# Attention's PSUM in two pools: the scores' two-bank tiles apart, the one-bank tiles and the product of P and V in one rotation of four

## The chip, the cores and the metric

The kernel runs on one core of a Trainium2 chip. The metric is the device time of one execution in microseconds (us). Five engines work beside each other and meet only at semaphores: TensorE (PE in the profile, with its weight loads as PEld), VectorE (DVE), ScalarE (ACT), GpSimd (POOL) and SyncE (SP), which issues the transfers. Matmuls write their results to PSUM, which the kernel uses as eight banks, each of 128 partitions by 512 fp32 numbers; DVE and ACT carry them from there to SBUF.

## What is computed

One layer of a hybrid block on 1024 latent tokens and 256 context tokens, width 1024, all in fp32. The part that the change touches is the window attention (8 query heads in two groups, blocks of 128 queries, three neighbouring key blocks and the context), which runs woven together with a bidirectional mLSTM and the output projection:

```python
s_loc = jnp.einsum('bnqhgd,bnkhd->bnhgqk', qb, kw).astype(jnp.float32) * scale
s_ctx = jnp.einsum('bnqhgd,bchd->bnhgqc', qb, kc).astype(jnp.float32) * scale
m = jnp.maximum(jnp.maximum(s_loc.max(-1, keepdims=True), s_ctx.max(-1, keepdims=True)), sk)
p_loc = jnp.exp(s_loc - m)
p_ctx = jnp.exp(s_ctx - m)
inv = 1.0 / (p_loc.sum(-1, keepdims=True) + p_ctx.sum(-1, keepdims=True) + jnp.exp(sk - m))
o = (jnp.einsum('bnhgqk,bnkhd->bnqhgd', (p_loc * inv).astype(v.dtype), vw)
     + jnp.einsum('bnhgqc,bchd->bnqhgd', (p_ctx * inv).astype(v.dtype), vc))
...
mix_x = jnp.concatenate([att_x, ml_x], axis=-1) @ w_out[layer]
x = x + gt_m * rms_norm(mix_x, g_post_mix[layer])
fx = swiglu(modulate(rms_norm(x, g_pre_ffn[layer]), sh_f, sc_f), w_ffn_in[layer], w_ffn_out[layer])
x = x + gt_f * rms_norm(fx, g_post_ffn[layer])
```

Before it come the modulation, the input projection and the mLSTM's states; behind it the output projection's rest and the feed-forward part.

## The kernel before

The attention stage runs through 16 items, one for each block of 128 queries (n from 0 to 7) and group of four heads (g 0 and 1). An iteration of the loop at L1038 works on three things at once. It computes the **scores** of the item two ahead (class `Soft`, four calls of `scores`, one a head: four matmuls, L953 and L954 twice, into a tile of tag "s", which takes two banks; DVE's L955 takes the maximum and moves the 512 or 640 columns out; ACT's L964 is the exponential, DVE's L966 the reciprocal, POOL's L969 the scaling). It transposes the **probabilities** of its own item (class `Values`, `tr`, up to five times T0 to T4: four transposes of 128 by 128, L982, fill one bank of tag "pt", which DVE's L985 (odd t) or ACT's L987 (even t) copies to SBUF as `ts_`). And, in the first eight iterations, it does one block of the **mLSTM**: `ml_scores` (L860, a tile of tag "s"), `ml_values` twice (L874 and L878 into two banks of tag "pt", read by DVE's L883 and L884 and by ACT's L890 in the first direction, DVE's L892 in the second), `ml_norm` (ACT, POOL's L902) and `ml_out` (four transposes L908 into a bank of tag "pt", read by DVE's L909). In odd iterations, when both groups' probabilities are transposed, `pv` multiplies them with V (L1000) into the bank `po`, and `pv_out` (ACT's L1006) copies that out. From the sixth iteration on the loop also casts the output weights (ACT's L925, POOL's L926), and at its end the output projection (L75 to L77 into tag "s") begins.

PSUM's eight banks in this stage are one pool: tag "s" has two tiles of two banks, "pt" three banks and "po" one. The product's bank `po` is used by nothing else until the feed-forward part. A tile that is asked for takes a bank of its tag that is free or comes free first, and its first matmul waits for the last reader of the tile that was there.

What stands where in each engine's queue is not written by hand in this stage: the program lists the steps of an iteration in the order of the strings `PLAN_ML`, `PLAN` and `PLAN13` (L35 to L37), and a scheduler then sets the order from its own estimate of when operands and banks are there. With `T` the transposes, `A` scores, `N` exponentials, `V` the values, `z` `ml_out`, `M` the product and `O` its copy:

```python
PLAN_ML = ("T0 A0 A1 A2 A3 T1 T2 T3 V0 N0 T4 z V1 w s N1 x p", "T0 A0 A1 A2 A3 T1 T2 V0 N0 T3 T4 z V1 w s M O N1 x p")
```

Only from the stage's last two items on (L1077 on) and in the whole feed-forward part is the order written by hand. Ahead of the attention, the pool `psA` holds the eight banks of the input projection; the last to leave them are the two halves of a sigmoid on ACT (L776), and `psB` opens in the same banks. The feed-forward part (L1118 on) goes on with tags "s", "pt" and "po".

Of the kernel before, what the change touches and what calls it, by code (L numbers as in the profile page):

```python
# [9 lines left out]
F32 = mybir.dt.float32  # L10
# [3 lines left out]
PSUM = bass.MemoryType.PSUM  # L14
ADD, SUB, MUL, MAX, MIN = ALU.add, ALU.subtract, ALU.mult, ALU.max, ALU.min

P = 128
D = 1024
# [24 lines left out]
def body(tc, x, ctx, vecs, bcv, bada, gqm, gqf, wada, ws1, ws2, wt, wout, wfi, wfo,  # L43
# [5 lines left out]
    def open_pool(name, bufs=1, side="left", space=None):  # L49
        kw = dict(name=name, bufs=bufs, reuse_waits="tile")  # L50
        if space is not None:
            kw["space"] = space
        else:
            kw["side"] = side
        p = tc.tile_pool(**kw)
        return p, p.__enter__()

    def close(p):
        p[0].__exit__(None, None, None)
# [65 lines left out]
    def R(k, name, shape, dt=F32):  # L125
        t = rp[1].tile([P, 1152 if k < 4 else 1024], dt, name=name, tag=f"r{k}")
        n = int(np.prod(shape))
        v = t[:, 0:n]
        if len(shape) == 2:
            v = v.rearrange("p (a b) -> p a b", b=shape[1])  # L130
        elif len(shape) == 3:
            v = v.rearrange("p (a b c) -> p a b c", b=shape[1], c=shape[2])
        elif len(shape) == 4:
            v = v.rearrange("p (a b c d) -> p a b c d", b=shape[1], c=shape[2], d=shape[3])
        return v
# [160 lines left out]
    for sec in (1, 0):  # L296
# [52 lines left out]
        for q in range(2):  # L349
            t = (hcol, scol)[sec][:, q]  # L350
# [70 lines left out]
    for i in range(NI):  # L421
# [16 lines left out]
        if i in (1, 2):  # L438
            b = i - 1
# [138 lines left out]
    def T(i, name):  # L578
        return q2.tile([P, S], F32, name=name, tag=f"s{i}")
# [159 lines left out]
    for j, name in enumerate(TILES):  # L739
# [10 lines left out]
        elif name == "ak":  # L750
# [5 lines left out]
            for a, b, w, dst in ((kr, ks, S, slice(0, S)), (kc[:, 0:L], kc[:, L:2 * L], L, slice(S, S + L))):  # L756
                t = th[64:P] if w == S else kc[64:P, 2 * L:3 * L]
# [7 lines left out]
        elif name.startswith("aq"):  # L765
            t = T(0, f"aq{i}")
# [6 lines left out]
        else:  # L773
            t = R(14 if i == 3 else 15, "so", (S,))
# [39 lines left out]
    pb = psB[1]  # L814
# [4 lines left out]
    qa = atp[1]  # L819
    qa.tile([P, 4, P], F32, name="ts_", tag="pts", bufs=NTS)  # L820
    qa.tile([P, 80], F32, name="padq")
    for x_, n in (("pt", 3), ("po", 1)):
        pb.tile([P, 4, P], F32, name=x_, tag=x_, bufs=n)

    def bank():
        return pb.tile([P, 4, P], F32, name="pt", tag="pt", bufs=3)

    def two_banks():
        return [t.rearrange("p a b -> p (a b)") for t in (bank(), pb.tile([P, 4, P], F32, name="po", tag="po", bufs=1))]


    wts, qps, hss, qz = {}, {}, {}, {}
# [71 lines left out]
    def ml_out(n):  # L904
        hs, so = hss.pop(n)
        pt = bank()
        for h in range(4):
            pe.transpose(pt[:, h, :], hs[:, h, :], ident)  # L908
        dve.tensor_tensor(mix[n][:, 4:8, :], pt, so, MUL)  # L909
# [79 lines left out]
    pos = {}  # L989

    def pv(a, b, ts, more, pin=True):

        ts = [t for t in ts if t < a.nt][::-1]
        first = a.n not in pos
        if first:
            pos[a.n] = pb.tile([P, 4, P], F32, name="po", tag="po", bufs=1)
        for t in ts:
            vt = a.kb0 + t if t < a.nb else NT + t - a.nb
            for g, x_ in ((1, b), (0, a)):
                r = pe.matmul(pos[a.n][64 * g:64 * g + 64], av[:, vt, g], x_.p.pop(t), start=first and t == ts[0],  # L1000
                              stop=not more and t == ts[-1])
                if pin and (t != ts[0] or not g):
                    tc.keep_in_program_order(r)

    def pv_out(n):
        act.copy(mix[n][:, 0:4, :], pos.pop(n))  # L1006
# [3 lines left out]
    for i in range(2):  # L1010
        a = Soft(i)
# [25 lines left out]
    b = None  # L1037
    for i in range(NIT):  # L1038
        a = Soft(i + 2) if i + 2 < NIT else None
        b0, b = b, Values(i)  # L1040
# [5 lines left out]
        for k in (PLAN_ML[i % 2] if i < NT else PLAN13 if i == NIT - 3 else PLAN[i % 2]).split():  # L1046
            op, n = k[0], int(k[1:] or 0)
            if op == "w" and i + 1 < NT:
                ml_load(i + 1)
            elif op == "T" and n < b.nt:  # L1050
                b.tr(n)
            elif op == "M" and i % 2:
                pv(b0, b, range(5), False)
            elif op == "O" and i % 2:
                pv_out(b.n)
            elif op == "A" and a:
                a.scores(n)
            elif op == "N" and a:
                a.norm(n)
            elif op == "V" and i < NT:  # L1060
                ml_values(i, n)
            elif op == "x" and i < NT:
                ml_norm(i)
            elif op == "s" and i + 1 < NT:
                ml_scores(i + 1)
            elif op == "z" and 1 <= i <= NT:
                ml_out(i - 1)
            elif op == "p" and i in WSPLIT:
                wout_split(i)
            elif op == "m":  # L1070
                msplit(0, 0)
                ops_[0] = pb.tile([P, 1024], F32, name="op", tag="s", bufs=2)
            elif op == "P":
                omm(0, 0, range(n, n + 1))
# [17 lines left out]
    msplit(1, 1)  # L1092
    act.preload_act_table_set("sqrt_and_others")
    pv(b, b2, range(4), False, False)
    omm(0, 1, range(3, 4))
    ops_[1] = pb.tile([P, 1024], F32, name="op", tag="s", bufs=2)
    omm(1, 1, range(4))
    pv_out(b.n)
    order.__exit__(None, None, None)
    close(atp)  # L1100
    close(aqp)
    close(akp)
# [142 lines left out]
    def mm_fi(ps, w, b, first):  # L1245

        for k in range(4):
            mm3(ps, (w[:, 0, k], w[:, 1, k]), b[k], first and k == 0, k == 3, more=not first)

    def bop(x):  # L1250
        return [(bh[x][0][:, k], bh[x][1][:, k]) for k in range(4)]

    xv, zb, tm_ = {}, {}, {}

    def fi1(p):
        if p == 2:
            xv[p] = two_banks()
        else:
            t = pb.tile([P, D], F32, name=f"xv{p}", tag="s", bufs=2)
            xv[p] = [t[:, 0:512], t[:, 512:D] if p else pb.tile([P, 512], F32, name="xv0b", tag="po", bufs=1)]  # L1260
        mm_fi(xv[p][0], wops[p]["11"], bop("11"), True)

    def fi2(p):
# [81 lines left out]
    tsums(2, (0, 1))  # L1345
    tsp("T2", 0, 2, "h")
    fi1(0)
    opost1(N1)
    es0 = prp[1].tile([P, 512], F32, name="es0", tag="mh", bufs=2)
# [7 lines left out]
    fi2(0)  # L1357
    xstore(N1)
    fi1(1)
    otr(N1)  # L1360
    close(pC)
# [20 lines left out]
    def fm(p, k):  # L1382

        w = wops[p]
        if k == 1:
            return fi1(p)
        if k == 2:
            return fi2(p)
        X = xv[p][0]
        if k == 6:  # L1390
            mm_fi(X, w["S2"], top("T2"), False)
        elif k == 5:
            zb[p] = bank().rearrange("p a b -> p (a b)")
            mm_fi(zb[p], w["S1"], top("T1"), True)
        elif k == 7:
            mm_fi(X, w["S3"], top("T3"), False)
        elif k == 4:
            mm_fi(X, w["22"], top("T4"), False)
        else:
            mm_fi(zb[p], w["S4"], bop("22"), False)  # L1400
# [95 lines left out]
    def gacc(k):  # L1496

        if k < KT:
            dve.scalar_tensor_tensor(gt["acc"], gt[k], csil[:, k, 0:1], gt["acc"], MUL, ADD)
            return  # L1500
        gps = two_banks()
        for i in range(2):
            sl = slice(i * 512, (i + 1) * 512)
            ps = gps[i]
            for p_ in range(2):
                pe.matmul(ps, gt["one"], gt["hl"][:, p_, sl], start=not p_, stop=p_ == 1)
            gt["p", i] = ps
# [193 lines left out]
    for p in range(4, HT):  # L1701
# [39 lines left out]
        if not end:  # L1741
            fm(p + 1, 1)
        else:
            X4 += two_banks()
            t = pb.tile([P, D], F32, name="fx2", tag="s", bufs=2)
            X4 += [t[:, 0:512], t[:, 512:D]]
            fstep(0)
# [95 lines left out]
    for s_ in range(1, 8):  # L1843
        q0 = (s_ - 1) * NJ
        KL = 4 if s_ == 7 else 2
        if s_ == 2:
            t = pb.tile([P, D], F32, name="fy0", tag="s", bufs=2)
# [35 lines left out]
    close(h2p)  # L1883
    close(prp)
    close(rp)
    close(psB)
    close(cp)

# [79 lines left out]
```

## Time and profile before

| | us |
|---|---|
| three timed runs | 1181.55, 1183.47, 1183.47 (median 1183.47) |
| the profiled execution, its own time | 1182.6 |
| its span from the first to the last instruction | 1180.8 |
| busy in the span: PE, DVE, ACT, POOL | 1161.4, 781.2, 558.2, 154.4 |
| the stage between the first score and the last copy of the product (L1006) | 292.8 to 459 |

Times within the span count from its start. PE starts a matmul before the one ahead of it has left the array, so that the rows of neighbouring matmuls overlap: what a matmul costs is the distance to the next one's start, not its own duration. An arrow in a row (`<-DVE ts__3367 L985`) names the instruction whose end released the waiting one, and the number before it is the idle time. A name such as `ts__3367` is one tile; its number differs between the two kernels by a small shift (before `pt_3369`, after `pt_3372`), as do line numbers behind L823 (before L982, after L987).

### The profile page before, as it was taken

To read this page: it belongs to the slowest core of one execution; us is meant where nothing else is said; L and a number is where in the kernel's file an instruction comes from. 1 tells how busy PE (TensorE), PEld (TensorE's weight loads), DVE (VectorE), ACT (ScalarE), POOL (GpSimd) and SP (SyncE) were. 2 spreads that over 40 slices of the span, in tenths; PEclk is the share of its full clock that TensorE was granted. 3 is DMA by queue.
4 is the path that set the end of the run, shared out by engine and by line. 5 is a ranking of instruction groups with operands and counts; after the bars stand their busy time and mean duration, and the time that the engine had idled before them with its cause. 6 is when DMAs were issued, how large, how long until landed. Compare 5 with 4: busy or idle time off the path is not lost.

```text
span 1180.8 us, 16205 instructions
## 1 busy us (share of the span) xinstructions
PE 1161.4 (98%) x5881; PEld 949.4 (80%) x5881; DVE 781.2 (66%) x1367; ACT 558.2 (47%) x1035; POOL 154.4 (13%) x204
## 2 busy tenths in 40 slices
PE   8899999999999999999999999999999999999997
PEld 3799888777777776888788888888888888888886
DVE  5863768872877752559767767777777755644566
ACT  6743442221776873887533433333333434434543
POOL 1550001225434670000000000000000000000000
PEclk9999999999999999999999999999999999999999
DMA  9611954748764325220333575655654458665853
GB/s 366 218 54 53 380 200 141 216 129 220 215 177 111 113 58 178 82 97 36 98 134 124 206 240 204 224 195 206 216 177 134 179 189 276 205 213 188 304 185 126
DMA packets 100264, 208.59 MB, mean 177 GB/s; under 512 B 9812, under 2 KB 39124, under 8 KB 98776
## 3 DMA queue, kind: packets, MB, share of 16 engines
q1 hardware_dynamic: 100184, 207.56, 52.9%
q8 instruction: 46, 0.75, 0.3%
q14 instruction: 34, 0.28, 0.1%
HBM read 154.04 MB, written 52.83 MB: 175 GB/s over the span
## 4 chain that ended last, share of the span: by engine, by line
PE 86%; DMA 5%; DVE 4%; issue 1%; ACT 1%; POOL 1%; SPq 1%; DVEq 0%; POOLq 0%; ACTq 0%
PE xv L77 8%; PE xv L75 8%; PE xv L76 8%; PE pt L75 6%; PE pt L76 6%; PE pt L77 6%; PE po L1000 3%; PE pt L982 3%; PE op L75 2%; PE op L77 2%; PE op L76 2%; PE t L595 2%; PE t L597 2%; PE t L594 2%; PE fx L75 2%; PE slab L75 2%
## 5 line engine op out<-in xcount | busy, mean ns | idle before, releaser
L64 DVE TENSOR_TENSOR fo<-fr,fo 128x1024 fp32r<-128x1024 f32 x77 | 92.6, 1222 | 69.8 <-ACT fo L63 65.4
L63 ACT CAST fo<-fr 128x1024 fp32r<-128x1024 f32 x77 | 79.7, 1052 | 73.9 <-PE pt L77 33.2
L594 PE MATMUL t<-hh,th 128*128 128x512 f32 x208 | 82.4, 396 | 0.0
L595 PE MATMUL t<-hl,th 128*128 128x512 f32 x208 | 82.1, 395 | 0.0
L1374 ACT CAST wS<-wr 128x512 fp32r<-128x512 f32 x88 | 54.2, 622 | 55.3 <-PE pt L77 36.7
L1376 DVE TENSOR_TENSOR wS<-wr,wS 128x512 fp32r<-128x512 f32 x88 | 60.4, 688 | 19.8 <-ACT wS L1374 19.7
L77 PE MATMUL xv<-tT,wS 128*128 128x512 f32 x168 | 65.7, 391 | 0.0
L75 PE MATMUL xv<-tT,wS 128*128 128x512 f32 x168 | 65.6, 391 | 0.0
L76 PE MATMUL xv<-tT,wS 128*128 128x512 f32 x168 | 65.5, 390 | 0.0
L597 PE MATMUL t<-hh,tl 128*128 128x512 f32 x208 | 65.0, 393 | 0.0
L75 PE MATMUL op<-woh,mh 128*128 128x512 f32 x128 | 51.0, 398 | 0.0
L77 PE MATMUL op<-woh,ml 128*128 128x512 f32 x128 | 49.9, 390 | 0.0
L76 PE MATMUL op<-wol,mh 128*128 128x512 f32 x128 | 49.9, 390 | 0.0
L1122 DVE TENSOR_TENSOR wr<-wr 128x512 f32<-128x512 f32 x66 | 45.5, 689 | 1.4
L594 PEld LDWEIGHTS t<-hh,th 128*128 128x128 f32 x208 | 39.1, 188 | 8.3 <-issue 0.3
L595 PEld LDWEIGHTS t<-hl,th 128*128 128x128 f32 x208 | 39.1, 188 | 8.1 <-issue 1.4
L1408 ACT ACTIVATE es<-es 128x512 f32<-128x512 f32 x22 | 13.9, 632 | 66.5 <-DVE es L1125 66.5
L953 PE MATMUL s<-k,qh 128*128 128x256 f32 (+1 forms) x128 | 42.7, 341 | 0.7 <-DVE sm L955 0.7
L75 PE MATMUL pt<-fo 128*128 128x512 f32 x110 | 42.8, 389 | 0.0
L77 PE MATMUL pt<-fo 128*128 128x512 f32 x110 | 42.8, 389 | 0.0
L76 PE MATMUL pt<-fo 128*128 128x512 f32 x110 | 42.8, 389 | 0.0
L597 PEld LDWEIGHTS t<-hh,tl 128*128 128x128 f32 x208 | 37.3, 188 | 6.6 <-issue 0.5
(784 smaller groups left out, 3344.5 us busy)
## 6 DMA issues: line engine op xcount, KB each, us to landing
wr<-in_wfi SPq DMA_DIRECT2D x44, 512.0 KB, 4.8
wb<-in_wada SPq DMA_DIRECT2D x24, 512.0 KB, 5.6
s_d<-a SPq DMA_DIRECT2D x22, 512.0 KB, 7.2
bt<-in_wfo SPq DMA_DIRECT2D x44, 256.0 KB, 3.9
tb_d<-bt SPq DMA_DIRECT2D x11, 1024.0 KB, 4.0
fr<-s_d SPq DMA_DIRECT2D x44, 256.0 KB, 4.2
fr<-tb_d SPq DMA_DIRECT2D x44, 256.0 KB, 4.3
fr<-a_d SPq DMA_DIRECT2D x33, 256.0 KB, 3.9
```

Source lines behind the costliest of these rows:

```text
L63: act.copy(hi, raw)
L64: dve.tensor_tensor(lo, raw, hi.bitcast(F32), SUB)
L75: pe.matmul(ps, a[0], b[0], start=first, stop=False, **kw)
L76: pe.matmul(ps, a[0], b[1], start=False, stop=False, **kw)
L77: pe.matmul(ps, a[1], b[0], start=False, stop=last, **kw)
L594: pe.matmul(o, wh[:, kt], m[0], start=f, stop=False)
L595: pe.matmul(o, wh[:, kt], m[1], start=False, stop=False)
L597: pe.matmul(o, wl[:, kt], m[0], start=False, stop=l)
L953: pe.matmul(o, qh[:, h, :], k2[g][:, kc], start=True, stop=False)
L1122: dve.tensor_tensor(out, a, b, SUB)
L1374: act.copy(w[:, 0], raw)
L1376: dve.tensor_tensor(w[:, 1], raw, w[:, 0].bitcast(F32), SUB)
```

## The change

The pool `psB` is left with tag "s" alone. A second pool, `psT`, opens with four one-bank tiles of tag "pt", and the product of P and V takes its bank from them like the transposes, the values and `ml_out`. When the attention ends, `psT` is closed and a pool `psT2` with three banks "pt" and one "po" takes its place for the feed-forward part, which asks for the same tiles as before.

```diff
--- before.py
+++ after.py
@@ -819,14 +819,19 @@
     qa = atp[1]
     qa.tile([P, 4, P], F32, name="ts_", tag="pts", bufs=NTS)
     qa.tile([P, 80], F32, name="padq")
-    for x_, n in (("pt", 3), ("po", 1)):
-        pb.tile([P, 4, P], F32, name=x_, tag=x_, bufs=n)
+    pb.tile([P, 1024], F32, name="s", tag="s", bufs=2)
+    psT = open_pool("psT", space=PSUM)
+    nbk = [4]
+    psT[1].tile([P, 4, P], F32, name="pt", tag="pt", bufs=4)
 
     def bank():
-        return pb.tile([P, 4, P], F32, name="pt", tag="pt", bufs=3)
+        return psT[1].tile([P, 4, P], F32, name="pt", tag="pt", bufs=nbk[0])
+
+    def po_bank():
+        return psT[1].tile([P, 4, P], F32, name="po", tag="po", bufs=1)
 
     def two_banks():
-        return [t.rearrange("p a b -> p (a b)") for t in (bank(), pb.tile([P, 4, P], F32, name="po", tag="po", bufs=1))]
+        return [t.rearrange("p a b -> p (a b)") for t in (bank(), po_bank())]
 
 
     wts, qps, hss, qz = {}, {}, {}, {}
@@ -993,7 +998,7 @@
         ts = [t for t in ts if t < a.nt][::-1]
         first = a.n not in pos
         if first:
-            pos[a.n] = pb.tile([P, 4, P], F32, name="po", tag="po", bufs=1)
+            pos[a.n] = bank()
         for t in ts:
             vt = a.kb0 + t if t < a.nb else NT + t - a.nb
             for g, x_ in ((1, b), (0, a)):
@@ -1097,6 +1102,11 @@
     omm(1, 1, range(4))
     pv_out(b.n)
     order.__exit__(None, None, None)
+    close(psT)
+    psT = open_pool("psT2", space=PSUM)
+    nbk[0] = 3
+    for x_, n in (("pt", 3), ("po", 1)):
+        psT[1].tile([P, 4, P], F32, name=x_, tag=x_, bufs=n)
     close(atp)
     close(aqp)
     close(akp)
@@ -1257,7 +1267,7 @@
             xv[p] = two_banks()
         else:
             t = pb.tile([P, D], F32, name=f"xv{p}", tag="s", bufs=2)
-            xv[p] = [t[:, 0:512], t[:, 512:D] if p else pb.tile([P, 512], F32, name="xv0b", tag="po", bufs=1)]
+            xv[p] = [t[:, 0:512], t[:, 512:D] if p else po_bank().rearrange("p a b -> p (a b)")]
         mm_fi(xv[p][0], wops[p]["11"], bop("11"), True)
 
     def fi2(p):
@@ -1883,6 +1893,7 @@
     close(h2p)
     close(prp)
     close(rp)
+    close(psT)
     close(psB)
     close(cp)
```

No engine's number of instructions changes. The order does, in the attention stage alone: the rows of PE ahead of the first score and from the feed-forward part on read the same.

**First place: PE in iteration 3 (block 1, group 1).** The rows are those around the last two transposes of an item's probabilities (`pt_3362` and `pt_3369` before, `pt_3365` and `pt_3372` after), the transposes of the mLSTM's output (`pt_3376`, after `pt_3379`) and the first bank of the second direction's values (`pt_3382`, after `pt_3385`); in brackets stands what the first row of a step waits for. Before:

```order
L878 MATMUL pt_3338<-V_88,wl3_3249 128x129 x2
L982 MATMUL pt_3362<-vec_59,pr__2974 128x128 [waits DVE_49]
L982 MATMUL pt_3362<-vec_59,pr__2974 128x128 x3
L982 MATMUL pt_3369<-vec_59,pr__2974 128x128 [waits DVE_49]
L982 MATMUL pt_3369<-vec_59,pr__2974 128x128 x3
L908 MATMUL pt_3376<-vec_59,hs2_3092 128x128 [waits Activation_49,Pool_49]
L908 MATMUL pt_3376<-vec_59,hs2_3092 128x128 x3
L874 MATMUL pt_3382<-cs2_2357,qz1_2937 128x129 [waits DMAHW4_49,Activation_49]
L874 MATMUL pt_3382<-cs2_2357,qz1_2937 128x129
L878 MATMUL pt_3382<-V_88,wl3_3249 128x129 x2
```

After:

```order
L987 MATMUL pt_3365<-vec_59,pr__2977 128x128 [waits Activation_49]
L987 MATMUL pt_3365<-vec_59,pr__2977 128x128 x3
L987 MATMUL pt_3372<-vec_59,pr__2977 128x128 [waits DVE_49]
L987 MATMUL pt_3372<-vec_59,pr__2977 128x128 x3
L958 MATMUL s_3469<-k2_0_1330,qh_3289 128x384 [waits DMAHW7_49,DMAHW0_49,DVE_49]
L959 MATMUL s_3469<-k2_0_1330,ql_3290 128x384 [waits DMAHW4_49,DMAHW3_49]
L958 MATMUL s_3469<-k2_0_1330,qh_3289 128x256
L959 MATMUL s_3469<-k2_0_1330,ql_3290 128x256
L913 MATMUL pt_3379<-vec_59,hs2_3095 128x128 [waits PE_49,DVE_49,Activation_49,Pool_49]
L913 MATMUL pt_3379<-vec_59,hs2_3095 128x128 x3
L879 MATMUL pt_3385<-cs2_2357,qz1_2940 128x129 [waits DVE_49,DMAHW1_49,PE_49,Activation_49]
L879 MATMUL pt_3385<-cs2_2357,qz1_2940 128x129
```

Before, both transposes wait for DVE, the second one for the copy of the first, whose bank it takes. After, the first waits for an earlier copy on ACT and the second for an earlier copy on DVE, and a score (`s_3469`) has moved in between them and the transposes of the mLSTM's output, which still wait for the values' bank (ACT's L890) and for POOL's L902.

**Second place: PE at the start of the attention.** The rows are the matmuls of the first two score tiles, behind the input projection. Before:

```order
L953 MATMUL s_2743<-k2_0_1330,qh_2312 128x256 [waits DMAHW3_49,DMAHW4_49,DVE_49,PE_49]
L954 MATMUL s_2743<-k2_0_1330,ql_2313 128x256 [waits DMAHW6_49,DMAHW5_49]
L953 MATMUL s_2743<-k2_0_1330,qh_2312 128x256
L954 MATMUL s_2743<-k2_0_1330,ql_2313 128x256
L953 MATMUL s_2749<-k2_0_1330,qh_2312 128x256
```

After:

```order
L958 MATMUL s_2746<-k2_0_1330,qh_2312 128x256 [waits DMAHW4_49,DMAHW3_49,Activation_49]
L959 MATMUL s_2746<-k2_0_1330,ql_2313 128x256 [waits DMAHW6_49,DMAHW5_49]
L958 MATMUL s_2746<-k2_0_1330,qh_2312 128x256
L959 MATMUL s_2746<-k2_0_1330,ql_2313 128x256
L958 MATMUL s_2752<-k2_0_1330,qh_2312 128x256
```

The order is the same. The first score waited for two transfers, DVE and PE; it now waits for two transfers and ACT, where the semaphore's value is that of the sigmoid L776 that reads the projection's last tile: the score tiles lie in other banks than before, and that tile was in one of them.

**Third place: PE where iteration 12 begins, near the stage's end.** The rows are those of three of the four scores of item 14 (`s_4469`, `s_4475`, `s_4481` before; `s_4472`, `s_4478`, `s_4484` after) and two transposes of item 12 (`pt_4462` and `pt_4493`). The fourth score and the product of P and V of iteration 11 follow on them in both kernels. Before:

```order
L953 MATMUL s_4469<-k2_0_1330,qh_4360 128x256
L954 MATMUL s_4469<-k2_0_1330,ql_4361 128x256
L953 MATMUL s_4469<-k2_0_1330,qh_4360 128x256
L954 MATMUL s_4469<-k2_0_1330,ql_4361 128x256
L982 MATMUL pt_4462<-vec_59,pr__4273 128x128 x4
L953 MATMUL s_4475<-k2_0_1330,qh_4360 128x256
L954 MATMUL s_4475<-k2_0_1330,ql_4361 128x256
L953 MATMUL s_4475<-k2_0_1330,qh_4360 128x256
L954 MATMUL s_4475<-k2_0_1330,ql_4361 128x256
L982 MATMUL pt_4493<-vec_59,pr__4273 128x128 x4
L953 MATMUL s_4481<-k2_0_1330,qh_4360 128x256
L954 MATMUL s_4481<-k2_0_1330,ql_4361 128x256
```

After:

```order
L958 MATMUL s_4472<-k2_0_1330,qh_4363 128x256
L959 MATMUL s_4472<-k2_0_1330,ql_4364 128x256
L958 MATMUL s_4472<-k2_0_1330,qh_4363 128x256
L959 MATMUL s_4472<-k2_0_1330,ql_4364 128x256
L958 MATMUL s_4478<-k2_0_1330,qh_4363 128x256
L959 MATMUL s_4478<-k2_0_1330,ql_4364 128x256
L958 MATMUL s_4478<-k2_0_1330,qh_4363 128x256
L959 MATMUL s_4478<-k2_0_1330,ql_4364 128x256
L958 MATMUL s_4484<-k2_0_1330,qh_4363 128x256
L959 MATMUL s_4484<-k2_0_1330,ql_4364 128x256
L958 MATMUL s_4484<-k2_0_1330,qh_4363 128x256
L959 MATMUL s_4484<-k2_0_1330,ql_4364 128x256
```

The two transposes that stood between the scores have moved behind the product of P and V, and the four scores now follow each other without other work between.

## The prediction

> **What bounds the kernel now.** The page comes first: the span, the engines' busy time and the chain that ended last.
>
> ```profile
> span 1180.8 us, 16205 instructions
> ...
> PE 1161.4 (98%) x5881; PEld 949.4 (80%) x5881; DVE 781.2 (66%) x1367; ACT 558.2 (47%) x1035; POOL 154.4 (13%) x204
> ...
> PE 86%; DMA 5%; DVE 4%; issue 1%; ACT 1%; POOL 1%; SPq 1%; DVEq 0%; POOLq 0%; ACTq 0%
> ```
>
> PE is busy for 98% of the span and carries 86% of the chain. The change alters neither the number nor the size of a matmul, so it can win only what PE loses in stops; and it reorders the attention stage alone (292.8 to 459 us). How much PE stops there is read from the windows of 20 us; the columns are the window, its length, then for PE, PEld, DVE, ACT and POOL the busy time with the number of instructions, then PE's granted clock.
>
> ```profile
> 300.00:320.00 20.00, 19.63 (x148) 16.03 (x147) 17.63 (x60) 15.45 (x46) 10.08 (x16) 1.00 0.81 214
> 320.00:340.00 20.00, 19.71 (x162) 18.62 (x160) 16.42 (x58) 14.77 (x46) 8.12 (x12) 1.00 0.73 195
> 340.00:360.00 20.00, 18.60 (x132) 14.09 (x130) 13.44 (x42) 12.19 (x35) 5.25 (x8) 1.00 0.50 130
> 360.00:380.00 20.00, 19.00 (x137) 14.47 (x136) 13.64 (x48) 14.54 (x43) 9.29 (x10) 1.00 0.47 117
> 380.00:400.00 20.00, 18.60 (x138) 15.26 (x138) 14.66 (x52) 15.08 (x47) 9.98 (x12) 1.00 0.32 99
> 400.00:420.00 20.00, 19.78 (x139) 15.44 (x136) 12.91 (x30) 16.03 (x32) 14.84 (x15) 1.00 0.43 117
> 420.00:440.00 20.00, 20.00 (x135) 15.72 (x134) 13.97 (x39) 17.99 (x41) 18.13 (x20) 1.00 0.25 69
> 440.00:460.00 20.00, 19.22 (x101) 11.67 (x100) 3.37 (x5) 5.32 (x8) 0.36 (x1) 1.00 0.45 159
> ```
>
> From 300 to 460 us PE is idle for 0.37 + 0.29 + 1.40 + 1.00 + 1.40 + 0.22 + 0.00 + 0.78 = 5.46 us. That is nearly all that there is to win, and 3.80 of it lies between 340 and 400. DVE is busy for 13 to 15 us of 20 there and ACT for 12 to 15, so neither is full. The list of PE's waits (300 to 460 us) names them; its columns are total, times, longest.
>
> ```profile
> PE pt L982 <- DVE ts__4019 L985: 0.8, 1, 0.8
> PE pt L982 <- DVE ts__3689 L985: 0.8, 1, 0.8
> PE pt L982 <- DVE ts__3367 L985: 0.8, 1, 0.8
> PE po L1000 <- DVE ts__4726 L985: 0.8, 1, 0.8
> PE pt L908 <- ACT hs L890: 0.7, 3, 0.2
> PE pt L908 <- POOL pr__3933 L942: 0.4, 1, 0.4
> PE pt L908 <- POOL pr__3603 L942: 0.4, 1, 0.4
> PE s L954 <- DMA ql<-aq_dl: 0.3, 1, 0.3
> ...
> PE pt L908 <- ACT ts__3221 L987: 0.2, 1, 0.2
> ```
>
> Except for two rows (the product waiting for data at the stage's end, `ts__4726`, and a transfer) these are waits of a transpose for a **bank** of tag "pt". How one comes about is in the timeline of iteration 3, PE's rows first, then DVE's and ACT's.
>
> ```profile
> 338.61 0.28 PE L954 MATMUL s<-k,ql 128*128 128x256 f32 x1
> 338.73 0.61 PE L874 MATMUL pt<-cs,qz 128*128 128x129 f32 x4
> ...
> 339.62 0.60 PE L982 MATMUL pt<-vec,pr__2974 128*128 128x128 f32 x4
> 341.00 0.66 PE L982 MATMUL pt<-vec,pr__2974 128*128 128x128 f32 x4 [0.78 <-DVE ts__3367 L985]
> 341.89 0.63 PE L908 MATMUL pt<-vec,hs 128*128 128x128 f32 x4 [0.23 <-ACT hs L890]
> ...
> 340.26 0.69 DVE L985 COPY ts__3367<-pt 128x512 f32<-128x512 f32 x1
> ...
> 341.12 1.14 ACT L890 ACTIVATE hs<-pt,dn 128x128 f32<-128x128 f32 x4 [2.10 <-DVE dn L885]
> ```
>
> T3 fills a bank at 339.62 to 340.22. The two banks of `ml_values` are still unread (ACT's L890 comes at 341.12), so T4 can only take the bank that T3 has just filled, and waits for DVE's whole copy of it (340.26, 0.69 long). Then L908 wants a bank of `ml_values` and waits for L890. A stop costs more than its idle time: a matmul's row lasts 0.28 us and the next begins 0.12 after it (338.61 to 338.73), so that each stop also loses the 0.16 by which the rows overlap.
>
> **The change part by part: what goes.** With four banks T4 no longer takes T3's (the first place of the order), and the product's bank `po`, idle between products, serves in between. The T4 waits of iterations 3, 5 and 7 (0.8 each in the list, 0.78 in the row above) cost 3 x (0.78 + 0.16) = 2.82. The three L908 waits right behind them (0.7 together) cost 0.7 + 3 x 0.16 = 1.18: in the new order some 2 us of work (the two transposes, `ml_scores` and a score) lie between the values and L908. In iterations 4 and 6 L908 waits once each, 0.4:
>
> ```profile
> 356.03 0.60 PE L982 MATMUL pt<-vec,pr__3130 128*128 128x128 f32 x4
> 357.02 0.63 PE L908 MATMUL pt<-vec,hs 128*128 128x128 f32 x4 [0.39 <-POOL pr__3603 L942]
> ...
> 356.29 1.14 ACT L890 ACTIVATE hs<-pt,dn 128x128 f32<-128x128 f32 x4 [3.37 <-PE pt L878]
> ```
>
> The row names POOL, but L942 only fills four columns; what L908 wants is a bank, and the first two of L890's four are through at about 356.9. In the changed order these transposes take banks that copies of earlier transposes have left: 2 x (0.39 + 0.16) = 1.10. The wait for `ts__3221` is 0.2 + 0.16 = 0.36. The sum of the banks' waits is 2.82 + 1.18 + 1.10 + 0.36 = **5.46**. The wait for `ql` (0.3 + 0.16) may go as well, since more work stands ahead of that score in the new order; it is worth between 0 and 0.46, and I take 0.2. Together 5.7.
>
> **What is added.** First the start (the second place of the order): the first score waits for the sigmoid that reads the projection's last tiles.
>
> ```profile
> 292.77 1.09 ACT L776 ACTIVATE so<-t 128x512 f32<-128x512 f32 x2 [6.40 <-PE t L597]
> ...
> 292.80 0.28 PE L953 MATMUL s<-k,qh 128*128 128x256 f32 x1
> ...
> 297.04 0.17 DVE L966 RECIPROCAL sm<-sm 128x2 f32<-128x2 f32 x1 [0.42 <-ACT pr__2740 L964]
> ...
> 298.05 1.21 PE L982 MATMUL pt<-vec,pr__2740 128*128 128x128 f32 x6 [0.58 <-POOL pr__2740 L969]
> ```
>
> The score moves from 292.80 to 293.86 (292.77 + 1.09), so 1.06 later, and DVE's four L955 and all other scores queue behind it. DVE's L966 had 0.42 of slack, so the first transposes, which wait for POOL's scaling behind it, come between 0.64 and 1.06 later; I take 0.9, since DVE is busy for 17.63 of the next 20 us and has little room to catch up.
>
> Then the runs of scores. With two tiles of tag "s", a third score waits until DVE has read the first.
>
> ```profile
> 424.56 0.73 DVE L955 CUSTOM_DVE_ANT_0 pr__4453<-s,mask,bcr 128x512 f32<-128x512 f32 x1
> ...
> 425.22 0.72 DVE L64 TENSOR_TENSOR ml<-mix,mh 128x512 fp32r<-128x512 f32 x1
> 425.86 0.74 DVE L955 CUSTOM_DVE_ANT_0 pr__4453<-s,mask,bcr 128x512 f32<-128x512 f32 x1
> ```
>
> DVE needs 0.66 for a score of item 14 (424.56 to 425.22) and has another 0.64 of L64 between; PE needs some 0.5 for its four matmuls (4 x 0.12). The two transposes that filled this time (0.43 each: the row of 0.60 above is three steps and a matmul of 0.28, so a step is 0.107) stand behind the product now (the third place of the order), so PE waits here for what they covered: between 0 (if DVE has got ahead) and 0.86; I take 0.7, nearer the upper end since DVE's queue is the same. A run of three scores in iteration 1 costs between 0 and 0.6 by the same reckoning with longer scores, taken at 0.4. The product of iteration 13 (`po_4624`) stood behind 24 matmuls of the output projection and now stands behind a transpose and one score, so that it waits for the copy of that transpose on ACT (0.57 to 0.59 at L987) less the score's 0.5, plus 0.16: between 0 and 0.6, taken at 0.3. One transpose tile there is split in two; 0.1 to 0.2.
>
> Finally the product's bank: in the rotation it is free again only after ACT's L1006.
>
> ```profile
> L1006 ACT COPY mix<-po x8: 579/586/587, 320.2 to 458.5; 128x512 f32<-128x512 f32 x8
> ...
>   PE po L1000: 13.0, 5
> ...
> 424.13 0.84 ACT L964 ACTIVATE pr__4357<-pr__4357,sm 128x641 f32<-128x641 f32 x1
> ```
>
> ACT takes 0.59 for it and sat waiting for the product in five of eight cases, so it is mostly there at once; what may stand ahead in its queue is exponentials, 0.84 each (the last row). Seven transposes in the new order take a bank that a product has left and wait for L1006; between the product and each of them stand three transposes and two scores, over 2 us (3 x 0.43 + 2 x 0.5), or 24 matmuls of the output projection. That hides the copy: I take 0; the end on the other side is the second rival.
>
> The costs are 0.9 + 0.7 + 0.4 + 0.3 + 0.15 = 2.45 (bounds 0.74 and 3.3), and the sum is 5.7 - 2.45 = **3.2 us** saved. Behind the stage nothing changes, and PE is at 20.00 of 20 us right behind it, so what is won there stays won. Against the profiled execution's 1182.6 (0.87 below the median of the three runs, and within them) that gives **1179.4**.
>
> **The rivals.** *The waits move.* A fourth bank doesn't make its readers faster. In the changed order L908 of iterations 3 and 5 still takes a bank of `ml_values`, and so waits for L890. If DVE's and ACT's queues reach the reciprocal and L890 as late as before, only T4 and the even L908 are won: 2.82 + 1.10 - 2.45 = 1.5, so 1181.1. For it: ACT waited 2.10 for the reciprocal in iteration 3, whose place in DVE's queue decides. Against it: DVE's copy that stood ahead of that reciprocal (340.26) now stands behind it. The Trainium skill (TensorEngine Tiling (Array Packing), "PSUM Bottleneck") says that a faster TensorE does not make the copies out of PSUM faster and that these may become the bottleneck. By that rule this rival would be the forecast; the windows agree with it for 420 to 440 us alone (ACT 17.99 of 20), and between 340 and 400 both copying engines are idle for a quarter of the time.
>
> *The product's bank is held* (slower). If ACT comes to L1006 only behind exponentials, the seven transposes stop PE, which had a bank of its own for the product before. With an exponential ahead and the copy, and no work hiding it, each stop is 0.84 + 0.59 + 0.16 = 1.59; seven are 11.1, and the sum is 7.9 slower, 1190.5; with half of it hidden 5.6, and 1185.0. It turns slower than before when a stop exceeds 3.2 / 7 = 0.46. Against it stand the 13.0 us that ACT waited for products.
>
> *The late stage takes the gain back.* From 417 to 434 us ACT works without a break. If PE comes 3 us earlier and ACT doesn't, PE waits for the copies of transposes, and the gain shrinks to what the stage's earlier idle ACT time gives: ACT is free for 3.97 us in 400 to 420, which is more than 3.2, so it should carry; if half of it is usable, 2 us remain, 1180.6.
>
> *The change doesn't do what it says.* Were the fourth bank never free when wanted, all bank waits would stay and the costs come: 1185. The order speaks against it, since T4 waits for an older copy there.
>
> **How the numbers follow.** What a measurement of this kernel can tell from no change is about 0.2%, or 2.4 us. Forecast (1177.5 to 1180.4): 0.58. The waits move: 0.21, and the late stage takes it back: 0.12, both around 1181. The bank is held, around 1185: 0.06. The change does nothing: 0.03. Faster by over 0.2% (below 1180.2) are nearly all of the forecast and a little of the late stage's, 0.57 in all; slower the last two, 0.09; same 0.34. The range reaches from the best case, 5.9 - 0.74 = 5.2 saved, 1177.4, and 0.6 less for runs that lie up to 1.9 apart, to 1183.1, where only T4's waits go and the costs take their upper bounds (2.82 - 3.3 = -0.5), and 0.4 more for the runs: 1176.8 to 1183.5.
>
> **What would show it.** Right: no wait of L982 for DVE between 335 and 400 us, PE's idle time in 340 to 400 down from 3.80 to under 1, the first score at about 293.9, a wait of a score for L955 near 421 to 424, and the last L1006 some 3 us earlier than 458.5. Wrong: waits of L908 for L890 as long as before (the first rival), waits of L982 for L1006 (the second), or copies at 417 to 434 that PE waits for (the third). A change of the time behind the attention would contradict the whole account.

## The result and the profile after

| | before | changed kernel |
|---|---|---|
| median, us (runs) | 1182.34 (1181.41 to 1183.47, 6) | 1178.09 (1177.71 to 1178.87, 6) |
| the profiled execution, its own time | 1182.6 | 1177.75 |
| its span | 1180.8 | 1175.9 |

The ratio is 0.9964, with a 95% interval from 0.9951 to 0.9977: the kernel is faster by 2.7 to 5.8 us, with 4.25 between the medians. Forecast were 3.2, for 1179.4, in a range from 1176.8 to 1183.5.

The page of the changed kernel, its head and its chain:

```profile
span 1175.9 us, 16202 instructions
...
PE 1157.9 (98%) x5881; PEld 947.9 (81%) x5881; DVE 780.5 (66%) x1367; ACT 558.1 (47%) x1035; POOL 154.4 (13%) x204
...
PE 93%; DVE 2%; DMA 2%; ACT 1%; issue 1%; SPq 0%; POOL 0%; DVEq 0%; POOLq 0%
```

The number of matmuls is the same, and the copying engines are as busy as before. How long the attention stage takes can be read from two rows of PE's timeline in each kernel, the projection's last pair of matmuls (L597) and the first matmul of the output projection behind the last product (L75). Before:

```profile
292.35 0.61 PE L597 MATMUL t<-hh,tl 128*128 128x512 f32 x2
...
458.35 0.50 PE L75 MATMUL op<-woh,mh 128*128 128x512 f32 x1
```

After:

```profile
292.07 0.61 PE L597 MATMUL t<-hh,tl 128*128 128x512 f32 x2
293.64 0.38 PE L958 MATMUL s<-k,qh 128*128 128x256 f32 x1 [0.95 <-ACT so L776]
...
453.50 0.50 PE L75 MATMUL op<-woh,mh 128*128 128x512 f32 x1
```

The stage took 166.00 us and takes 161.43, which is 4.57 less; the span is 4.9 shorter, of which 0.28 had come about before the stage began. Behind it nothing changed. This length of the stage is used below beside the times, because it is the finer measure: the same program profiled on two occasions (e2_seam and e2_again) gave 160.39 and 160.40, while its medians were 1.07 apart. Of the kernel before and of the changed kernel there is one profile each.

PE's waits in the changed kernel (285 to 470 us; total, times, longest), against the list of before in the prediction:

```profile
PE s L958 <- DVE sm L960: 2.8, 4, 1.1
PE s L958 <- ACT so L776: 0.9, 1, 0.9
PE pt L1005 <- DVE ts__4729 L990: 0.9, 1, 0.9
PE pt L913 <- POOL hs L907: 0.3, 1, 0.3
PE s L865 <- DVE sm L960: 0.3, 1, 0.3
PE pt L1005 <- ACT ts__4614 L992: 0.2, 1, 0.2
```

In the kernel before, the same stretch, which begins earlier than the list in the prediction, also had:

```profile
PE s L953 <- DVE sm L955: 0.7, 2, 0.5
```

Every wait of a transpose for a bank has gone, as has that for `ql`. New are the wait for L776 and longer waits of scores for DVE's L960 (before L955), 2.8 against 0.7. Nothing waits for L1011 (before L1006), the product's copy. In iteration 3, PE's rows around T3 and T4 now read:

```profile
336.70 0.61 PE L883 MATMUL pt<-V,wl 128*128 128x129 f32 x4
337.24 0.71 PE L865 MATMUL s<-mq,mk 64*128 64x128 f32 x8
337.89 1.09 PE L987 MATMUL pt<-vec,pr__2977 128*128 128x128 f32 x8
338.74 0.42 PE L958 MATMUL s<-k,qh 128*128 128x384 f32 x1
...
339.58 0.66 PE L913 MATMUL pt<-vec,hs 128*128 128x128 f32 x4
```

T3 and T4 are one row of eight transposes, and 2.4 us of other work lie between the values' end and L913, which finds its bank free. The windows from 340 to 400 show where the idle time was, and what is left of it:

```profile
340.00:360.00 20.00, 20.00 (x154) 16.25 (x152) 14.91 (x52) 12.92 (x39) 7.16 (x10) 1.00 0.50 147
360.00:380.00 20.00, 19.71 (x149) 15.97 (x148) 14.64 (x48) 13.83 (x41) 9.47 (x11) 1.00 0.48 120
380.00:400.00 20.00, 18.86 (x140) 15.38 (x139) 13.90 (x49) 17.56 (x51) 12.78 (x13) 1.00 0.31 88
```

PE's idle time there fell from 3.80 to 1.43, and 1.15 of that is one stop that the prediction did not have:

```profile
385.73 1.03 PE L987 MATMUL pt<-vec,pr__3606 128*128 128x128 f32 x8
387.91 0.44 PE L958 MATMUL s<-k,qh 128*128 128x384 f32 x1 [1.15 <-DVE sm L960]
...
388.60 0.60 PE L913 MATMUL pt<-vec,hs 128*128 128x128 f32 x4
```

DVE's rows at that place:

```profile
386.36 0.69 DVE L990 COPY ts__4022<-pt 128x512 f32<-128x512 f32 x1 [0.32 <-PE pt L987]
386.97 0.88 DVE L960 CUSTOM_DVE_ANT_0 pr__4090<-s,mask,bcr 128x640 f32<-128x640 f32 x1
387.77 0.08 DVE L960 DVE_READ_ACCUMULATOR2_ANT sm<- 128x1 f32 x1
```

Two scores of item 10 had been run ahead of T3 and T4 of item 7. DVE cannot take them out before T4 has left item 7's probabilities, since only three buffers of these exist, and the copy of T3 stands ahead of it as well. Here the two end close together: T4's row ends at 386.76, and DVE goes from the copy straight to L960 at 386.97. So the third score finds both score tiles full until 387.85 (387.77 + 0.08).

### The profile page after: what moved, and what is told of

Same layout as the page of the kernel before. It is cut to its first block, busy times and chain, and to the rows that moved or that the text cites. A ratio compares the mean times of both kernels' runs of the same rounds, so it can differ in the third digit from the quotient of the medians.

```text
span 1175.9 us, 16202 instructions
## 1 busy us (share of the span) xinstructions
PE 1157.9 (98%) x5881; PEld 947.9 (81%) x5881; DVE 780.5 (66%) x1367; ACT 558.1 (47%) x1035; POOL 154.4 (13%) x204
## 4 chain that ended last, share of the span: by engine, by line
PE 93%; DVE 2%; DMA 2%; ACT 1%; issue 1%; SPq 0%; POOL 0%; DVEq 0%; POOLq 0%
PE xv L77 8%; PE xv L75 8%; PE xv L76 8%; PE pt L77 6%; PE pt L75 6%; PE pt L76 6%; PE t L595 4%; PE t L594 4%; PE t L597 4%; PE pt L1005 3%; PE op L75 3%; PE op L77 2%; PE op L76 2%; PE pt L987 2%; PE fx L75 2%; PE slab L75 2%
## 5 line engine op out<-in xcount | busy, mean ns | idle before, releaser
L75 PE MATMUL xv<-tT,wS 128*128 128x512 f32 x168 | 65.6, 391 | 0.0
L597 PE MATMUL t<-hh,tl 128*128 128x512 f32 x208 | 65.0, 393 | 0.0
L75 PE MATMUL op<-woh,mh 128*128 128x512 f32 x128 | 51.0, 398 | 0.0
L75 PE MATMUL pt<-fo 128*128 128x512 f32 x110 | 42.8, 389 | 0.0
L597 PEld LDWEIGHTS t<-hh,tl 128*128 128x128 f32 x208 | 37.3, 188 | 6.6 <-issue 0.5
```

Source lines behind the costliest of these rows:

```text
L75: pe.matmul(ps, a[0], b[0], start=first, stop=False, **kw)
L597: pe.matmul(o, wl[:, kt], m[0], start=False, stop=l)
```

## The experiments

All times are medians; the kernel before was run beside them, in three groups (1182.69 beside e1 to e7, 1182.22 beside e8 and e9, 1181.89 beside e10_dve and e2_again). "Stage" is the length read as above. In these kernels line numbers lie up to four further on than in the changed kernel.

| run | median, us | ratio to before, 95% interval | stage, us |
|---|---|---|---|
| before | | | 166.00 |
| changed kernel | 1178.09 | 0.9964, 0.9951 to 0.9977 | 161.43 |
| e1_split | 1183.02 | 1.0001, 0.9993 to 1.0010 | 166.22 |
| e2_seam | 1176.90 | 0.9954, 0.9940 to 0.9967 | 160.39 |
| e2_again | 1177.97 | 0.9964, 0.9951 to 0.9978 | 160.40 |
| e3_three | 1184.41 | 1.0018, 1.0009 to 1.0027 | 167.90 |
| e7_z_po | 1178.98 | 0.9971, 0.9961 to 0.9981 | 162.47 |
| e8_late | 1177.63 | 0.9964, 0.9950 to 0.9977 | 160.94 |
| e9_cast | 1177.67 | 0.9960, 0.9947 to 0.9972 | 160.42 |
| e9b_casts | 1184.98 | 1.0026, 1.0012 to 1.0039 | 167.82 |
| e10_dve | 1176.44 | 0.9952, 0.9939 to 0.9964 | 159.73 |

### The split alone: e1_split

```diff
-    nbk = [4]
-    psT[1].tile([P, 4, P], F32, name="pt", tag="pt", bufs=4)
+    nbk = [3]
+    for x_, n in (("pt", 3), ("po", 1)):
+        psT[1].tile([P, 4, P], F32, name=x_, tag=x_, bufs=n)
...
-            pos[a.n] = bank()
+            pos[a.n] = po_bank()
```

> The pools are split and the scores' tiles take the changed kernel's banks, but the single banks stay three, with one more for the product; every engine's queue keeps the order of the kernel before. Theory (the fourth bank in the rotation brings the gain, the scores' new banks cost a wait at the start): the three T4 waits of 0.8 and the five L908 waits stay, the first score waits 0.95 for L776, and the time is that of the kernel before plus 0.5 to 1.1, about 1183. Rival (the split itself, or where the tiles lie, brings the gain): the time is near that of the changed kernel, 1178 to 1179.

The three T4 waits are there (0.8 each in its list of waits), with 0.9 for L776:

```profile
PE s L959 <- ACT so L776: 0.9, 1, 0.9
PE pt L988 <- DVE ts__4023 L991: 0.8, 1, 0.8
PE pt L988 <- DVE ts__3371 L991: 0.8, 1, 0.8
PE pt L988 <- DVE ts__3693 L991: 0.8, 1, 0.8
```

The time is the one of before, and the stage 0.22 longer. So the split and the scores' new banks bring nothing by themselves, and the rival falls. The expected 0.5 to 1.1 for the start was too much in this order: PE starts 1.11 late, but the first transposes then wait 0.50 less for POOL (the gap in front of them falls from 0.86 to 0.36), and the wait for `ql`, 0.51 with its lost overlap, is not there, since that transfer lands in the meantime.

### The scores' tiles in their old banks: e2_seam

```diff
-    psB = open_pool("psB", space=PSUM)
+    p = tc.tile_pool(name="psB", bufs=1, reuse_waits="tile", space=PSUM, side="right")
+    psB = (p, p.__enter__())
```

> The changed kernel with its scores' tiles at the other end of PSUM, in the banks that they had before; every engine's queue keeps the order of the changed kernel. Theory (the start's wait for L776 costs, net of what POOL and DVE hid): no wait for L776, the first transposes 0.4 to 0.7 earlier, and the time 0.5 to 1.1 below the changed kernel, 1177.0 to 1177.6. Rival (the start is held by POOL's and DVE's chain, and the wait was hidden): the first transposes and the time stay within 0.2 of the changed kernel.

> e2_seam once more, beside e10_dve on the same chip: 1176.3 to 1177.7, its earlier run.

No queue's order differs from the changed kernel's, and the wait for L776 is gone. The stage is 1.04 shorter in the first run and 1.03 in the second, at the upper end of what was expected. Counted from the stage's start, the first transposes come 1.0 earlier, where 0.4 to 0.7 were expected: less of the wait had been hidden than thought. In the changed kernel little else hides the start's wait: that for `ql` had already gone with the new order, and POOL writes the first columns of the probabilities sooner (0.98 behind the stage's start in e2_seam, at L948, and 2.91 in the kernel before, at L942). The times (1176.90 and 1177.97 against 1178.09) do not show it by themselves: the first lies 0.1 below the range expected of it and the second 0.3 above its own.

### Three banks in the rotation: e3_three

```diff
-    nbk = [4]
-    psT[1].tile([P, 4, P], F32, name="pt", tag="pt", bufs=4)
+    nbk = [3]
+    psT[1].tile([P, 4, P], F32, name="pt", tag="pt", bufs=3)
```

> The changed kernel with three single banks in the rotation instead of four, the product's among them; one bank of PSUM is left unused in this stage. Theory (it is the number of banks): the T4 waits of 0.8 are back, and while the product holds a bank only two are left, so more waits of L908 and of the values' banks come; slower than the kernel before by 1 to 5, 1183 to 1187. Rival (what counts is that the product's bank isn't reserved, since it lay idle between products): no slower than the kernel before, 1179 to 1182.

The first rows of its waits that concern banks:

```profile
PE pt L987 <- DVE ts__3370 L990: 0.8, 1, 0.8
PE pt L987 <- DVE ts__4022 L990: 0.8, 1, 0.8
PE pt L987 <- DVE ts__3692 L990: 0.8, 1, 0.8
...
PE pt L913 <- ACT ts__3544 L992: 0.8, 1, 0.8
PE pt L913 <- ACT ts__3870 L992: 0.8, 1, 0.8
PE pt L913 <- ACT hs L895: 0.7, 3, 0.2
PE pt L879 <- ACT hs L895: 0.6, 1, 0.6
```

All of the waits for banks are back, those of L913 in iterations 4 and 6 twice as long (0.8 for 0.4), and there is one of the values. The stage is 1.90 longer than before, and 1.68 longer than that of e1_split, where the start waits for L776 too. It is the number of banks, and sharing the product's bank alone does not do it.

### The mLSTM's output in the product's bank: e7_z_po

```diff
 def ml_out(n):
     hs, so = hss.pop(n)
-    pt = bank()
+    pt = po_bank()
```

This stands on e1_split: three banks in the rotation, the fourth shared by the product and `ml_out`.

> The pools split as in e1_split, three single banks and one more, but the transposes of the mLSTM's output (L908) take the product's bank instead of one of the three. Theory (each wait is for a bank of its own kind): the five L908 waits go (2.3 with their lost overlap), the three T4 waits of 0.8 stay, and the time is 1.5 to 2.5 below e1_split. Rival (T4 and L908 wait for the same thing, the scheduler's order, and only the whole rotation frees them): within 0.8 of e1_split.

The time is 4.0 below e1_split and the stage 3.75, far more than the 2.3 that the L908 waits were worth. The T4 waits went too, though T4 still takes T3's bank (at 340.83 the values' two banks are unread, since ACT's L896 begins at 340.90). PE in iteration 3:

```profile
339.40 0.60 PE L988 MATMUL pt<-vec,pr__2978 128*128 128x128 f32 x4
340.33 0.66 PE L914 MATMUL po<-vec,hs 128*128 128x128 f32 x4 [0.33 <-POOL hs L908]
340.83 0.62 PE L988 MATMUL pt<-vec,pr__2978 128*128 128x128 f32 x4
```

The transposes of the mLSTM's output (L914), which no longer need a bank of the rotation, stand between T3 and T4 and cover the copy that T4 waits for. They wait for POOL's L908 instead, in three iterations, 1.6 together.

Both expectations missed: the gain is larger than either had it. That each wait belongs to a bank of its own is wrong: T4 and L908 waited for one shortage, and a free bank for L908's transposes lets them fill the time of T4's copy. Whether a free bank for T4 would do the same was not tried. A fixed home in the product's idle bank already brings 3.75 of the 4.79 that lie between e1_split and the changed kernel.

### The new stop in iteration 7: e8_late, e9_cast, e9b_casts, e10_dve

All four stand on e2_seam, whose stop near 385 is the one at 386.5 of the changed kernel. In e8_late the third score of item 10 is ordered behind L908:

```diff
-            pe.transpose(pt[:, h, :], hs[:, h, :], ident)
+            zlast[0] = pe.transpose(pt[:, h, :], hs[:, h, :], ident).ins
...
-                pe.matmul(o, qh[:, h, :], k2[g][:, kc], start=True, stop=False)
+                r = pe.matmul(o, qh[:, h, :], k2[g][:, kc], start=True, stop=False)
+                if self.i == 10 and h == 2:
+                    tc.add_manual_dep(r.ins, zlast[0].name, mybir.DependencyInfo(mybir.DependencyClass.NoSync, mybir.DependencyReason.DATA), reason="late")
```

> e2_seam with the third score of item 10 ordered behind the transposes of the mLSTM's output (L908) of iteration 7; in the changed kernel that score stands ahead of them and stops PE for 1.39 at 386.5, because both score tiles are full until DVE's L955, which waits for T4 of item 7 to leave the probabilities' buffer. Rival (the score's place costs what it stops): the stop goes and the time falls by 1.0 to 1.4 against e2_seam, to 1175.6 or so. Theory (L908 behind it is not ready either: POOL's L902 for it ends at 388.45 in the changed kernel, when L908 starts at 388.60): PE stops in front of L908 instead, about as long, and the time is within 0.6 of e2_seam.

PE stops in front of L914 (before L908) instead, for POOL:

```profile
387.51 0.66 PE L914 MATMUL pt<-vec,hs 128*128 128x128 f32 x4 [1.74 <-POOL hs L908]
```

The stop grows from 1.15 to 1.74 and the stage by 0.55. The score's place was not what it cost; the score had filled a part of the time until POOL is through.

> e2_seam with the cast of one output weight (ACT's L925, 1.03, in iteration 6) free to go earlier: it leaves its place ahead of iteration 7's L890 and goes 26 rows earlier in ACT's queue; PE's order stays. Theory (PE's stop in iteration 7 is for DVE and POOL, not for ACT): the stop of a score near 385 stays at 1.2 to 1.4 and the time is within 0.5 of e2_seam. Rival (ACT's late L890 is what iteration 7 is late by): the stop shrinks by 0.5 or more and the time falls by 0.5 to 1.

```diff
-        tc.keep_in_program_order(act.copy(h, raw))
+        r = act.copy(h, raw)
+        if i != 6:
+            tc.keep_in_program_order(r)
```

The cast that stood at 384.55 in e2_seam has gone from there: no cast runs between 371 and 395. The stop stays at 1.15 and the stage at 160.42: ACT's cast is not on the path there.

> e2_seam with all eight casts of the output weights on ACT free to go where the scheduler puts them; they go one iteration earlier mostly, and PE's order changes in a few places of iterations 6 to 13. Theory: casts are not on the path, so only the changed order counts; within 1.0 of e2_seam, on either side. Rival (ACT's queue sets the late stage): 1 to 2 below e2_seam.

```diff
-        tc.keep_in_program_order(act.copy(h, raw))
+        act.copy(h, raw)
```

Neither was right: it is 7.4 longer in the stage. In ACT's queue casts now stand where their weights have not landed (four of the eight wait, 9.8 together), and everything behind them waits, the copies of transposes among them; PE waits for those. Two of the four in ACT's rows:

```profile
405.33 1.04 ACT L931 CAST woh<-wor 128x1024 fp32r<-128x1024 f32 x1 [2.52 <-DMA wor<-in_wout]
406.29 0.58 ACT L993 COPY ts__4253<-pt 128x512 f32<-128x512 f32 x1
...
420.72 1.05 ACT L931 CAST woh<-wor 128x1024 fp32r<-128x1024 f32 x1 [3.19 <-DMA wor<-in_wout]
```

PE's rows of the products that wait for them:

```profile
406.92 0.64 PE L1006 MATMUL pt<-ts__4253,av 128*64 128x512 f32 x1 [1.12 <-ACT ts__4253 L993]
...
424.40 1.12 PE L1006 MATMUL pt<-ts__4433,av 128*64 128x512 f32 x1 [2.58 <-ACT ts__4433 L993]
```

The second stop costs more than its length. The matmuls behind it are slower at first (1.12 for a row, where 0.64 and 0.59 are usual), and the windows show why; the number in front of the last two is PE's granted clock.

```profile
424.00:426.00 2.00, 1.60 (x4) 0.53 (x6) 2.00 (x6) 2.00 (x5) 1.57 (x2) 0.50 0.18 72
...
428.00:430.00 2.00, 2.00 (x12) 0.56 (x8) 0.12 (x1) 0.85 (x1) 2.00 (x2) 1.00 0.00 0
```

Towards the end of the stop the granted clock fell to half, and it was back at full by 428. The product's first four pairs of matmuls took 3.20 (424.40 to 427.60), where the changed kernel's took 1.77 (420.07 to 421.84), so 1.4 more. None of the other profiles here shows the clock below full within the stage; their longest stop is the 1.74 of e8_late. With the overlap that they also lose, the two stops in the rows cost 1.2 and 2.65, and a stop of the values behind a third cast (0.80 at 379.83) 0.95. With the clock's 1.4 that is 6.2 of the 7.4; the rest was not traced.

In e10_dve `ml_norm`'s last product goes from POOL to DVE:

```diff
-        pool.tensor_tensor(hs, hs, hcast(sq), MUL)
+        dve.tensor_tensor(hs, hs, hcast(sq), MUL)
```

> e2_seam with ml_norm's last product (L902, 1.04 on POOL, eight times) on DVE; the scheduler then puts the third score of item 10 behind L908 and the values by itself. Theory (iteration 7's stop is POOL's late L902, as e8_late showed): no wait for L902 is left, the stop near 385 falls from 1.39 to 0.9 or less (L908 takes the bank of T3 and waits for its copy), and DVE's eight extra products of about 0.7 lie in its idle time: 0.3 to 1.0 below e2_seam of the same call. Rival (DVE is the fuller engine in 300 to 340, 16 to 18 of 20 us, and hands the time back as waits of scores for L955): 0.3 to 2 above it.

The stage is 0.67 shorter than that of e2_again, within what was expected; the medians, 1176.44 and 1177.97, are further apart than the stage explains. Its two waits of L914:

```profile
PE pt L914 <- DVE ts__4022 L991: 1.1, 1, 1.1
...
PE pt L914 <- DVE hs L908: 0.5, 1, 0.5
```

The wait for POOL is gone, but the stop of iteration 7 only falls from 1.39 to 1.27 with its lost overlap, and not to 0.9: L914 takes the bank of T3 and waits for its copy, as forecast, and that copy (386.48) now stands behind the moved product in DVE's queue (385.37, 1.18 long). So that stop gives little of the gain, and the expectation missed its size. One wait for the moved product is left (0.5, in iteration 1), where the third score had stopped PE about as long. The stops of L908 in iterations 3 and 5 (0.17 and 0.45 in the changed kernel) have gone, and they are most of the gain. The eight products take DVE time that it has: it is busy for 15.5 to 17.0 of 20 us between 320 and 400. This version takes 0.9952 of the time before, and its stage is 1.70 shorter than the changed kernel's.

## Why the prediction was right, and where it was off

**The banks' waits, 5.46.** By the distances between starts they were 3 x 0.95 (T4), 0.39 + 0.38 + 0.39 and 0.55 + 0.56 (L908) and 0.34: 5.46, and all are gone. That four banks remove them and three do not is shown by e1_split and e3_three. Of the sum 0.6 came back as waits of L913 for POOL (0.45 and 0.17), as the first rival had it in small, though for POOL's L907 and not for L890. What was wrong was to sum the waits as separate things: e7_z_po removes all of them with one of the two uses moved, and has 1.6 of waits for POOL in their place.

**The wait for `ql`** went entirely (0.51); 0.2 had been taken.

**The start, 0.9** (0.64 to 1.06): 1.04 in the changed kernel's order, by e2_seam. It would have been 0.22 in the order of before, by e1_split, where a transfer and POOL hid most of it.

**The runs of scores.** At the beginning of iteration 12 PE lost 0.70 more than before, as forecast (at 418.67, where 421 to 424 had been named). In iteration 1 it lost 0.81, twice what had been taken (0.4) and above its upper bound of 0.6. Ahead of the first of these scores (read at 313.86) DVE had a copy of transposes (L990 at 313.12, 0.69) and a row of the mLSTM (L888). The step that failed is the bound: it was carried over from iteration 12 and did not ask what stands in DVE's queue here.

**The product of iteration 13** lost 0.27, where 0.3 had been taken.

**What no term had** is the stop at 386.5, 1.39 with its lost overlap, while a smaller one of before, 0.47 in front of a score at 406.12, went. Because of it one sign of the prediction did not come: PE's idle time from 340 to 400 fell to 1.43, and not under 1. The prediction looked for runs of scores and overlooked that of scores running ahead of T4, which hold both tiles until T4 is through. By e8_late, the stop would be there in another place, since POOL was not through with L902.

**On the other side,** more than half of the gain is in none of these stops. The gains named are 5.46 + 0.51 + 0.47, and 0.42 of shorter waits of the very first transposes in the new order (read in e2_seam, without the start's wait): 6.86. The costs are 1.04 + 0.81 + 1.39 + 0.70 + 0.27 and the 0.6 that came back: 4.8. That leaves 2.1 of the 4.57. The other 2.5 lie in steps of 0.2 at most between the kinds of work, and 1.0 of them can be read from PE's rows. Before, two of the eight `ml_scores` (L860) were split by transposes; the rows are those of iteration 4:

```profile
350.49 0.49 PE L860 MATMUL s<-mq,mk 64*128 64x128 f32 x2
350.91 1.09 PE L982 MATMUL pt<-vec,pr__3130 128*128 128x128 f32 x8
351.93 0.71 PE L860 MATMUL s<-mq,mk 64*128 64x128 f32 x6
352.57 0.66 PE L982 MATMUL pt<-vec,pr__3130 128*128 128x128 f32 x4
```

In the changed kernel none is split:

```profile
350.97 0.71 PE L865 MATMUL s<-mq,mk 64*128 64x128 f32 x8
351.62 0.45 PE L958 MATMUL s<-k,qh 128*128 128x384 f32 x1
```

The two parts take 0.42 and 0.64, a whole one 0.65, and the step into the second part is 0.20 where transposes follow each other at 0.11: 0.5 for each split. What the other 1.5 come from was not tried and stays open.

So the forecast's mechanism was right and its size 1.1 (by the medians) to 1.4 (by the stage) too small: a missed stop and a run sized too small cost more than the sum had, and small steps that it left out made more than that good. That it came out this near is partly luck.

**The rivals.** The product's bank is not held: no instruction waits for L1011. The late stage does not take the gain back; e9b_casts shows, though, that ACT's queue there has little to spare, since casts that waited 2.5 to 3.5 for their weights there, with the lowered clock behind one of the stops, account for 6.2 of the 7.4 by which its stage is longer. The rule that copies out of PSUM may become the bottleneck when TensorE gets faster (the Trainium skill, TensorEngine Tiling (Array Packing), "PSUM Bottleneck") does not describe this stage: with more banks, PE went from 56.2 to 58.6 busy of the 60 us between 340 and 400, DVE stayed under 15 of 20 and ACT came near full in the last window alone (17.56).

## What to carry to other kernels

A bank that is reserved for something rare is worth a look at the moment when a transpose must take the bank that was filled just before: there the whole copy stands open (0.78 of idle time here). A bank for other work that can run meanwhile, as in e7_z_po, or one more in the rotation lets the scheduler fill it. When a pool is moved to other banks, look who leaves those banks last; here it cost 1.04 of the 5.6 that could be had, and one argument put it right. A wait may stand in front of the next thing that is late (e8_late): move it in an experiment before counting on what it costs.

## What had not been expected of the hardware

The length of a stage repeats far better than the time of the whole program: 160.39 and 160.40 in two profiles of one program, whose profiled executions took 1176.31 and 1177.51 because the stage began at 291.8 and 292.9; e9_cast, with the same order on PE, gave 160.42. For a change inside one stage, the stage's length resolved differences of 0.1 us that the times cannot.

An instruction at the head of a queue that waits for a transfer cost far more than its own 1.05 (e9b_casts): ACT sat idle for 2.52 and 3.19, and PE waited 1.1 and 2.6 for copies behind it. And the longer of these stops took PE's granted clock with it, which was seen this once: the clock was at 0.50 from about 423.9 to 427.3, so that the matmuls behind the stop ran at half speed and cost another 1.4, while e8_late's stop of 1.74 was followed by transposes at their usual pace (L914 to L880 in 0.50).
